# Low parts of the next stage's weights by accumulating transfers, and transposes moved later, in a float32 network of attention, delta-rule and feed-forward layers

## The chip, the cores and the metric

The kernel runs on one core of a Trainium2 chip. The metric is the device time of one execution in microseconds (us). The engines are PE (TensorE, matrix products), DVE (VectorE), ACT (ScalarE), POOL (GpSimd) and SP (SyncE, which only issues transfers here). Transfers are issued from SP's queue and from POOL's queue and run on the core's 16 DMA engines.

## What is computed

A small decoder over 512 tokens of width 1024, in float32. Two layers come first: a mixer (two kinds of attention in the first layer, differential attention in the second) and a feed-forward block with a gated convolution, each between two root-mean-square norms. Then come a gated delta-rule mixer, a squared-ReLU feed-forward block and a last norm.

```python
for layer in range(DEPTH):
    h = _rms_norm(x, norm_mix_pre[layer])
    m = _even_mixer(h, ...) if layer % 2 == 0 else _odd_mixer(h, ...)
    x = x + _rms_norm(m, norm_mix_post[layer])
    h = _rms_norm(x, norm_ffn_pre[layer])
    f = _conv_ffn(h, ffn_w_up[layer], ffn_conv_w[layer], ffn_conv_b[layer], ffn_w_down[layer])
    x = x + _rms_norm(f, norm_ffn_post[layer])
...
y = gated_deltanet(rms_norm(x, norm_mix), ...)
x = x + y
x = x + squared_relu_mlp(rms_norm(x, norm_mlp), mlp_w_up, mlp_w_down)
return rms_norm(x, norm_final)
```

## The kernel before

**Three products for one.** A float32 product is made of three products of parts: each operand is split into a high part (`hi`, the value cast to `fp32r`) and a low part (`lo`, the value less `hi`). `mm3` issues high by high, high by low, low by high, at lines 250 to 252; when the weight is the first operand, line 252 reads its low part and comes third.

**Weights.** `wtile` loads 128x1024 numbers (512 KB) into one of two buffers `raw` (`wload`, line 230, on SP's queue). `wsteps` then casts `raw` to `whi` on ACT (line 245) and makes `wlo = raw - whi` on DVE, or on POOL where `eng` says so (line 246). `whi` and `wlo` have four buffers each, used in turn. A buffer of `raw` can be loaded again when both the cast and the subtraction have read it.

**The five stage ends.** The tokens are four blocks t = 0 to 3 of 128. At the end of a stage each block is finished (norm and addition to x), scaled by the next norm (`scale`, a sum of squares on ACT; `rstd`, a power on POOL, line 265; `mul`, on DVE, line 293), transposed on PE (`turn`, line 301) and split into `hT`, high on ACT and low on DVE (`parts`). The next stage begins with a head: its first four weights W0 to W3, in `steps` that need only blocks 0 and 1. So PE works on the head while blocks 2 and 3 are made ready, and their `turn`s are put between the steps.

- `proj_out` ends the three mixers (even, odd, delta rule). Its head has 32 steps of three products, eight for each weight in turn, and `turn(2)` follows step 24, `turn(3)` step 29 (counted from 0). W0 and W3 get their low parts on POOL, W1 and W2 on DVE. W0 takes the buffers of the output projection's weight k=4, which is read last by the first two of the products of `block(3)`.
- `ffn_tail` ends the two gated feed-forward blocks. The down projection there is seven products of combined quarters (class `Seven`); products 3 to 6, each with two halves b of four `mm` (2.7 us of PE), are interleaved by hand with the norms. Its four weights come after product 6's first half, with low parts on DVE. Its head has 16 steps (first block) or 32 (second); `turn(2)` follows step 13 or 27, `turn(3)` the last. The residual is read back block by block (`reload`, SP's queue) into three buffers `scr`, which the scaled blocks use as well.

Around both the order of PE, ACT and DVE is the program's own (`manual_schedule`). SP's and POOL's orders are the planner's. Each engine works in order: an instruction that waits holds all behind it on its engine. Within class `Seven`, transfers on POOL's queue already add a quarter of the weights to another as they land (`accum_op=ALU.add`, line 96).

Of the kernel before, what the change touches and what calls it, by code (L numbers as in the profile page):

```python
# [10 lines left out]
F32 = mybir.dt.float32  # L11
F32R = mybir.dt.float32r
# [3 lines left out]
ALU = mybir.AluOpType  # L16
# [5 lines left out]
P = 128  # L22
# [115 lines left out]
def parts(hi, lo):  # L138

    return lambda k, t: (hi[:, k, t * P:(t + 1) * P], lo[:, k, t * P:(t + 1) * P])  # L140


class Kern:
# [92 lines left out]
    def wsplit(self, raw, n=1024, eng=None):  # L236
        parts, lo = self.wsteps(raw, n, eng)
        lo()
        return parts

    def wsteps(self, raw, n=1024, eng=None):

        hi = self.wp.tile([P, 1024], F32R, tag="whi", name="whi", bufs=4)
        lo = self.wp.tile([P, 1024], F32R, tag="wlo", name="wlo", bufs=4)
        self.nc.scalar.copy(hi[:, :n], raw[:, :n])  # L245
        return (hi, lo), lambda: (eng or self.nc.vector).tensor_tensor(lo[:, :n], raw[:, :n], hi.bitcast(F32)[:, :n], ALU.subtract)  # L246
# [27 lines left out]
    def scale(self, t):  # L274

        ss = self.sm([P, 1], "pn_ss")
        self.nc.scalar.activation(self.junk(), self.x[:, t, :], AF.Square, accum_out=ss)
        return self.rstd(ss, D, "pn_r")
# [90 lines left out]
    def proj_out(self, out, finish, nxt=None, tail=4):  # L369

        nc = self.nc
        nk = out.nk
        body = nk - tail
        lead = min(2, body)
        for h in (1, 0):
            for k in range(lead):
                for t in range(NT):
                    out.mm(k, t, h)  # L380
        for k in range(lead, body):
            for h in range(2):
                for t in range(NT):
                    out.mm(k, t, h)
        for k in range(body, nk):
            out.weight(k)
        order = [(k, h) for k in range(body, nk) for h in range(2)]

        def block(t, i0=0, i1=2 * tail):
            for k, h in order[i0:i1]:  # L390
                out.mm(k, t, h)

        banks = lambda t: (out.bank(0, t), out.bank(1, t))
        if not isinstance(nxt, tuple):
            for t in range(NT):
                if t:
                    order.sort(key=lambda kh: kh[1])
                block(t)
                if nxt:
                    nxt(t, banks(t))  # L400
                    continue
                for step in finish:
                    step(t, banks(t))
            return

        i, (srcs, run) = nxt
        f_scale, f_mul, f_add = (lambda t, f=f: f(t, banks(t)) for f in finish)
        E = mybir.EngineType
        scale, mul, turn, parts = self.prenorm(i)
        ws2 = []  # L410

        def weight(eng=None):
            if len(ws2) < len(srcs):
                ws2.append(self.wtile(*srcs[len(ws2)], eng=eng))

        with self.tc.manual_schedule(engines={E.PE, E.Activation, E.DVE}):
            block(0)
            f_scale(0)
            f_mul(0)
            block(1)  # L420
            f_add(0)
            scale(0)
            mul(0)
            f_scale(1)
            f_mul(1)
            f_add(1)
            block(2, 0, 3)
            turn(0)
            block(2, 3)
            parts(0)  # L430
            scale(1)
            mul(1)
            f_scale(2)
            f_mul(2)
            block(3, 0, 3)
            weight(nc.gpsimd)
            turn(1)
            block(3, 3)
            parts(1)
            weight()  # L440
            f_add(2)
            f_scale(3)
            scale(2)
            f_mul(3)
            weight()
            weight(nc.gpsimd)
            mul(2)
            f_add(3)
            scale(3)
            mul(3)  # L450
            steps = run(ws2)
            n = len(steps)
            for j, step in enumerate(steps):
                step()
                if j == n * 3 // 4:
                    turn(2)
                    parts(2)
                if j == n * 29 // 32:
                    turn(3)
                    parts(3)  # L460

# [860 lines left out]
    def ffn_tail(self, down, spare, put, xd, gain_row, nxt):  # L1322


        nc = self.nc
        i, (srcs, run) = nxt
        gain = self.gain(gain_row)
        E = mybir.EngineType
        scale, mul, turn, parts = self.prenorm(i, "bb")
        col = lambda h: slice(h * 512, h * 512 + 512)  # L1330
        ws2, xr, st = [], {}, {}

        def weight(eng=None):
            if len(ws2) < len(srcs):
                ws2.append(self.wtile(*srcs[len(ws2)], eng=eng))

        def reload(t):
            xr[t] = self.scr("xr")
            nc.sync.dma_start(xr[t], xd[:, t, :])

        def square(t, h):
            if t not in st:
                st[t] = self.sm([P, 2], "po_ss")
            nc.scalar.activation(self.junk()[:, col(h)], self.x[:, t, col(h)], AF.Square, accum_out=st[t][:, h:h + 1])

        def gained(t, h):
            nc.vector.tensor_tensor(self.x[:, t, col(h)], self.x[:, t, col(h)], gain[:, col(h)], ALU.mult)

        def half(t, h):
            square(t, h)  # L1350
            gained(t, h)

        def root(t):
            sum_ = self.sm([P, 1], "po_st")
            nc.vector.tensor_tensor(sum_, st[t][:, 0:1], st[t][:, 1:2], ALU.add)
            st[t] = self.rstd(sum_, D, "po_r")

        def add(t):
            nc.vector.scalar_tensor_tensor(self.x[:, t, :], self.x[:, t, :], st[t], xr[t], ALU.mult, ALU.add)

        def rest(b):

            put(*down.sums(5, b)[:2], 0, 1)

        def pairs(i, b, j0, j1):
            for j in range(j0, j1):
                down.mm(i, j, b)

        with self.tc.manual_schedule(engines={E.PE, E.Activation, E.DVE}):
            down.apart = True  # L1370
            down.weights(4)
            reload(0)
            reload(1)
            five, six = down.weights(5, spare[0]), down.weights(6, spare[1])
            for step in five:
                step()
            half(0, 0)
            down.block(3, 0)
            put(*down.sums(3, 0))
            down.block(4, 0)  # L1380
            put(*down.sums(4, 0))
            half(0, 1)
            six[0]()
            root(0)
            down.block(3, 1)
            put(*down.sums(3, 1))
            add(0)
            down.block(4, 1)
            put(*down.sums(4, 1))
            six[1]()  # L1390
            scale(0)
            half(1, 0)
            half(1, 1)
            mul(0)
            root(1)
            down.block(5, 0)
            put(*down.sums(5, 0))
            rest(0)
            add(1)
            down.block(5, 1)  # L1400
            turn(0)
            put(*down.sums(5, 1))
            parts(0)
            scale(1)
            reload(2)
            mul(1)
            rest(1)
            down.block(6, 0)
            weight()
            pairs(6, 1, 0, 2)  # L1410
            turn(1)
            pairs(6, 1, 2, 4)
            put(*down.sums(6, 0))
            parts(1)
            half(2, 1)
            weight()
            half(2, 0)
            root(2)
            reload(3)
            weight()  # L1420
            add(2)
            put(*down.sums(6, 1))
            half(3, 1)
            half(3, 0)
            root(3)
            scale(2)
            add(3)
            weight()
            mul(2)
            scale(3)  # L1430
            mul(3)
            steps = run(ws2)
            n = len(steps)
            for j, step in enumerate(steps):
                step()
                if j == n * 27 // 32:
                    turn(2)
                    parts(2)
                if j == n - 1:
                    turn(3)  # L1440
                    parts(3)
# [736 lines left out]
```

## Time and profile before

| | us |
|---|---|
| median of 3 runs (lowest, highest) | 1913.55 (1913.24, 1917.69) |
| the profiled execution, its own time | 1912.77 |
| its span in the trace | 1911.0 |
| PE busy (share of the span) | 1869.3 (98%) |
| DVE busy | 1229.3 (64%) |
| ACT busy | 906.1 (47%) |
| POOL busy | 314.1 (16%) |

The span is the time from the first to the last instruction in the trace. Busy time is a sum over instructions, and PE's ends are modelled. Times in the rows below count from the span's start. In a timeline a row has the start, the duration, the engine, the line, the operation with its output and inputs, its shape, how many were merged, and in brackets how long the engine sat idle before it and what ended that. The even mixer ends near 300 us, the first feed-forward block near 645 us, the odd mixer near 885 us, the second feed-forward block near 1240 us and the delta-rule mixer near 1586 us.

### The profile page before, as it was taken

What the parts mean: (1) busy time and instruction counts of PE and PEld (TensorE: products, weight loads), DVE (VectorE), ACT (ScalarE), POOL (GpSimd) and SP (SyncE); (2) the same over time, 40 slices, a digit from 0 to 9 for tenths busy, and PEclk for the clock granted to TensorE, in tenths of its full rate; (3) what the DMA queues carried; (4) which work ended last, traced back from release to release, by engine and by line L of the source; (5) the groups of instructions that cost most, each with busy time, mean ns of one, the idle gap of its engine ahead of it and who ended that gap; (6) DMA issues with size and microseconds to landing.
All of it is one profiled execution on the core that took longest, in us unless ns stands there. A gap on an engine that the chain in (4) does not pass through costs nothing.

```text
span 1911.0 us, 25424 instructions
## 1 busy us (share of the span) xinstructions
PE 1869.3 (98%) x9732; PEld 1542.6 (81%) x9732; DVE 1229.3 (64%) x1959; ACT 906.1 (47%) x1453; POOL 314.1 (16%) x412
## 2 busy tenths in 40 slices
PE   7999999999999999999999999999999999999998
PEld 6778688888888788878888888788778879888886
DVE  5666656565657647847555666877763747766767
ACT  4665644343434546645343344476622424444444
POOL 0212420100101223412010100100264311100101
PEclk9999999999999999999999999999999999999999
DMA  5212146453734321127363543523330146746553
GB/s 175 63 52 82 45 147 211 105 190 94 183 109 78 129 68 57 65 89 249 103 190 110 128 160 80 151 84 101 97 98 4 45 132 203 194 111 198 125 140 88
DMA packets 66046, 226.01 MB, mean 118 GB/s; under 512 B 8788, under 2 KB 9684, under 8 KB 65796
## 3 DMA queue, kind: packets, MB, share of 16 engines
q1 hardware_dynamic: 52948, 181.77, 27.8%
q0 software_dynamic: 12976, 42.61, 12.7%
q8 instruction: 77, 1.26, 0.3%
q14 instruction: 45, 0.37, 0.1%
HBM read 214.32 MB, written 9.96 MB: 117 GB/s over the span
## 4 chain that ended last, share of the span: by engine, by line
PE 51%; DVE 3%; ACT 1%; issue 1%; DMA 1%; POOL 1%; POOLq 0%; ACTq 0%; DVEq 0%
PE up L250 3%; PE up L251 3%; PE up L252 3%; PE X L250 2%; PE X L251 2%; PE X L252 2%; PE dproj L250 2%; PE gate L252 2%; PE val L252 2%; PE gate L251 2%; PE val L251 2%; PE gate L250 2%; PE val L250 2%; PE dproj L251 2%; PE dproj L252 2%; PE Z L251 1%
## 5 line engine op out<-in xcount | busy, mean ns | idle before, releaser
L246 DVE TENSOR_TENSOR wlo<-raw,whi 128x1024 fp32r<-128x1024 f32 (+2 forms) x205 | 250.9, 1228 | 170.0 <-ACT whi L245 163.6
L245 ACT CAST whi<-raw 128x1024 fp32r<-128x1024 f32 (+3 forms) x225 | 234.0, 1042 | 239.6 <-PE gate L251 54.1
L245 ACT CAST whi<-quarter 128x1024 fp32r<-128x1024 f32 (+1 forms) x132 | 132.6, 1008 | 182.9 <-PE X L252 48.6
L246 DVE TENSOR_TENSOR wlo<-quarter,whi 128x1024 fp32r<-128x1024 f32 (+1 forms) x132 | 153.4, 1166 | 89.7 <-ACT whi L245 89.3
L96 POOL DMA_DIRECT2D quarter<-in_ff_wq x48 | 41.7, 880 | 590.0 <-DVE wlo L246 480.4
L250 PE MATMUL gate<-hhi,whi 128*128 128x512 f32 x320 | 124.5, 389 | 0.0
L251 PE MATMUL gate<-hlo,whi 128*128 128x512 f32 x320 | 124.5, 389 | 0.0
L252 PE MATMUL gate<-hhi,wlo 128*128 128x512 f32 x320 | 124.5, 389 | 0.0
L250 PE MATMUL val<-hhi,whi 128*128 128x512 f32 x320 | 124.5, 389 | 0.0
L251 PE MATMUL val<-hlo,whi 128*128 128x512 f32 x320 | 124.5, 389 | 0.0
L252 PE MATMUL val<-hhi,wlo 128*128 128x512 f32 x320 | 124.5, 389 | 0.0
L226 DVE TENSOR_TENSOR mlo<-q,mhi 128x1792 fp32r<-128x1792 f32 x38 | 77.0, 2026 | 58.3 <-ACT mhi L225 58.3
L250 PE MATMUL X<-whi,mhi 128*128 128x512 f32 x272 | 106.1, 390 | 0.0
L251 PE MATMUL X<-wlo,mhi 128*128 128x512 f32 x272 | 105.8, 389 | 0.0
L252 PE MATMUL X<-whi,mlo 128*128 128x512 f32 x272 | 105.4, 389 | 0.0
L225 ACT CAST mhi<-q 128x1792 fp32r<-128x1792 f32 x38 | 64.4, 1696 | 77.7 <-DVE q L1928 67.1
L250 PE MATMUL up<-hhi,whi 128*128 128x512 f32 x224 | 87.1, 389 | 0.0
L251 PE MATMUL up<-hlo,whi 128*128 128x512 f32 x224 | 87.1, 389 | 0.0
L252 PE MATMUL up<-hhi,wlo 128*128 128x512 f32 x224 | 87.1, 389 | 0.0
L252 PE MATMUL head<-hhi,wlo 128*128 128x256 f32 (+1 forms) x256 | 73.0, 287 | 1.9 <-DVE wlo L246 1.5
L250 PE MATMUL head<-hhi,whi 128*128 128x256 f32 (+1 forms) x256 | 71.9, 287 | 1.3 <-ACT whi L245 1.0
L251 PE MATMUL head<-hlo,whi 128*128 128x256 f32 (+1 forms) x256 | 72.7, 285 | 0.1
(461 smaller groups left out, 4856.1 us busy)
## 6 DMA issues: line engine op xcount, KB each, us to landing
raw<-in_ff_wup SPq DMA_DIRECT2D x88, 512.0 KB, 3.5
quarter<-in_ff_wq SPq DMA_DIRECT2D x40, 512.0 KB, 5.2
quarter<-in_ff_wq POOLq DMA_DIRECT2D x40, 512.0 KB, 5.5
raw<-in_ml_wup SPq DMA_DIRECT2D x32, 512.0 KB, 3.5
quarter<-in_ml_wdown SPq DMA_DIRECT2D x32, 512.0 KB, 6.4
quarter<-in_ml_wdown POOLq DMA_DIRECT2D x32, 512.0 KB, 5.5
raw<-in_dn_wqkv SPq DMA_DIRECT2D x24, 512.0 KB, 3.7
raw<-in_od_wqk SPq DMA_DIRECT2D x16, 512.0 KB, 3.4
```

Of the source, the lines that this page charges most:

```text
L96: self.K.nc.gpsimd.dma_start(r[quarter][:, :src[other].shape[-1]], src[other], accum_op=ALU.add)
L225: i = self.nc.scalar.copy(hi, src)
L226: return i.ins, (eng or self.nc.vector).tensor_tensor(lo, src, hi.bitcast(F32), ALU.subtract).ins
L245: self.nc.scalar.copy(hi[:, :n], raw[:, :n])
L246: return (hi, lo), lambda: (eng or self.nc.vector).tensor_tensor(lo[:, :n], raw[:, :n], hi.bitcast(F32)[:, :n], ALU.subtract)
L250: mm(out, lhs[0], rhs[0], start=start, stop=False, **kw)
L251: mm(out, lhs[0], rhs[1], start=False, stop=False, **kw)
L252: return mm(out, lhs[1], rhs[0], start=False, stop=stop, **kw)
```

## The change

A new function `wtile_dma` makes a weight's low part without a subtraction on an engine: ACT casts `raw` to `hi`, ACT writes `-hi` into `lo`, and a transfer on POOL's queue adds the weight, read from memory a second time, onto `lo` as it lands. `raw` is then free as soon as the cast has read it. `proj_out` uses it for W0 and W3, in place of POOL's subtraction; `ffn_tail` uses it for all four weights, in place of DVE's, and calls for them earlier (W0 after `root(0)`, W1 after block 1's squares, W2 after `add(1)`, W3 after `rest(1)`). In `proj_out`, `turn(2)` moves from step 24 to step 27 and `turn(3)` from step 29 to step 31, the last. In `ffn_tail`, one `mm` of product 6 more stands ahead of `turn(0)`, and one more ahead of `turn(1)`, so that one `mm` in place of two follows it.

```diff
+    def wtile_dma(self, src, n=1024):
+
+        raw = self.wload(src, n)
+        hi = self.wp.tile([P, 1024], F32R, tag="whi", name="whi", bufs=4)
+        lo = self.wp.tile([P, 1024], F32R, tag="wlo", name="wlo", bufs=4)
+        self.nc.scalar.copy(hi[:, :n], raw[:, :n])
+        self.nc.scalar.mul(lo[:, :n], hi.bitcast(F32)[:, :n], -1.0)
+        self.nc.gpsimd.dma_start(lo[:, :n], src, accum_op=ALU.add)
+        return hi, lo
+
@@ proj_out
-        def weight(eng=None):
+        def weight(make=self.wtile):
             if len(ws2) < len(srcs):
-                ws2.append(self.wtile(*srcs[len(ws2)], eng=eng))
+                ws2.append(make(*srcs[len(ws2)]))
...
             block(3, 0, 3)
-            weight(nc.gpsimd)
+            weight(self.wtile_dma)
             turn(1)
             block(3, 3)
             parts(1)
...
             weight()
-            weight(nc.gpsimd)
+            weight(self.wtile_dma)
             mul(2)
             f_add(3)
...
-                if j == n * 3 // 4:
+                if j == n * 27 // 32:
                     turn(2)
                     parts(2)
-                if j == n * 29 // 32:
+                if j == n - 1:
                     turn(3)
                     parts(3)
@@ ffn_tail
-        def weight(eng=None):
+        def weight():
             if len(ws2) < len(srcs):
-                ws2.append(self.wtile(*srcs[len(ws2)], eng=eng))
+                ws2.append(self.wtile_dma(*srcs[len(ws2)]))
...
             half(0, 1)
             six[0]()
             root(0)
+            weight()
             down.block(3, 1)
...
             half(1, 0)
             half(1, 1)
+            weight()
             mul(0)
             root(1)
             down.block(5, 0)
             put(*down.sums(5, 0))
             rest(0)
             add(1)
+            weight()
             down.block(5, 1)
+            pairs(6, 0, 0, 1)
             turn(0)
             put(*down.sums(5, 1))
             parts(0)
...
             reload(2)
             mul(1)
             rest(1)
-            down.block(6, 0)
             weight()
-            pairs(6, 1, 0, 2)
+            pairs(6, 0, 1, 4)
+            pairs(6, 1, 0, 3)
             turn(1)
-            pairs(6, 1, 2, 4)
+            pairs(6, 1, 3, 4)
             put(*down.sums(6, 0))
             parts(1)
             half(2, 1)
-            weight()
             half(2, 0)
             root(2)
             reload(3)
-            weight()
             add(2)
...
             add(3)
-            weight()
             mul(2)
```

## Rows read from the trace of the kernel before

**Rows 1.** Windows of the span: busy times of each engine, clock, DMA share, GB/s.

```profile
300.00:600.00 300.00, 300.00 (x1331) 248.52 (x1330) 182.08 (x216) 124.38 (x135) 18.13 (x21) 1.00 0.49 134
```

**Rows 2.** Waits of PE over the span: total us, times, longest us.

```profile
PE pn_t L301 <- DVE nrm L293: 15.0, 9, 7.9
...
PE head L252 <- DVE wlo L246: 1.5, 1, 1.5
...
PE head L250 <- ACT whi L245: 1.0, 1, 1.0
```

**Rows 3.** Timeline of PE at the end of the first feed-forward block.

```profile
619.10 1.09 PE L301 MATMUL pn_t<-ident,nrm 128*128 128x128 f32 x8 [0.34 <-DVE nrm L293]
...
625.70 1.07 PE L301 MATMUL pn_t<-ident,nrm 128*128 128x128 f32 x8 [1.39 <-DVE nrm L293]
...
637.89 0.50 PE L250 MATMUL headb<-whi,hhi 128*128 128x512 f32 x1 [1.49 <-ACT whi L245]
639.90 0.67 PE L251 MATMUL headb<-wlo,hhi 128*128 128x512 f32 x1 [1.51 <-DVE wlo L246]
```

**Rows 4.** Windows around the low clock at the two feed-forward ends (columns of rows 1).

```profile
637.00:643.00 6.00, 3.61 (x11) 2.70 (x12) 4.94 (x6) 1.99 (x3) 1.44 (x3) 0.76 0.55 186
1232.00:1238.00 6.00, 4.04 (x21) 3.84 (x22) 4.95 (x5) 1.89 (x4) 1.00 (x2) 0.72 0.75 303
```

**Rows 5.** Timelines of ACT and DVE at the even mixer's end.

```profile
270.54 1.06 ACT L245 CAST whi<-raw 128x1024 fp32r<-128x1024 f32 x1 [0.67 <-PE o L252]
...
280.66 1.05 ACT L245 CAST whi<-raw 128x1024 fp32r<-128x1024 f32 x1 [2.10 <-DMA raw<-in_ff_wup]
...
273.88 1.28 DVE L246 TENSOR_TENSOR wlo<-raw,whi 128x1024 fp32r<-128x1024 f32 x1 [0.31 <-ACT whi L245]
```

**Rows 6.** Timeline of PE at the even mixer's end.

```profile
275.55 0.28 PE L252 MATMUL head<-hhi,wlo 128*128 128x256 f32 x1
...
284.82 0.38 PE L252 MATMUL head<-hhi,wlo 128*128 128x256 f32 x1 [0.47 <-POOL wlo L246]
...
288.27 1.09 PE L301 MATMUL pn_t<-ident,nrm 128*128 128x128 f32 x8 [0.40 <-DVE nrm L293]
```

**Rows 7.** POOL's 30 accumulating transfers of 512 KB between 1610 and 1900 us.

```profile
DMA to landing us min/median/max: 5.3/5.5/8.5
```

**Rows 8.** POOL's accumulating transfers issued in 283:287 and 1581:1583 (last column: us to landing).

```profile
quarter<-in_ff_wq POOLq DMA_DIRECT2D x1, 512.0 KB, 9.5
...
quarter<-in_ml_wdown POOLq DMA_DIRECT2D x1, 512.0 KB, 9.7
```

**Rows 9.** Timelines of ACT, DVE, POOL and PE at the odd mixer's end.

```profile
874.69 1.05 ACT L245 CAST whi<-raw 128x1024 fp32r<-128x1024 f32 x1 [0.96 <-DMA raw<-in_ff_wup]
...
876.11 3.42 DVE L334 SCALAR_TENSOR_TENSOR x<-post,po_rr,x 128x1024 f32<-128x1024 f32 x1
...
875.82 2.63 POOL L246 TENSOR_TENSOR wlo<-raw,whi 128x1024 fp32r<-128x1024 f32 x1 [3.09 <-ACT whi L245]
...
869.88 0.28 PE L252 MATMUL head<-hhi,wlo 128*128 128x256 f32 x1
...
883.05 1.09 PE L301 MATMUL pn_t<-ident,nrm 128*128 128x128 f32 x8 [1.50 <-DVE nrm L293]
```

**Rows 10.** Timelines of ACT and PE at the delta-rule mixer's end.

```profile
1578.57 1.05 ACT L245 CAST whi<-raw 128x1024 fp32r<-128x1024 f32 x1 [1.95 <-DMA raw<-in_ml_wup]
...
1573.49 0.28 PE L252 MATMUL head<-hhi,wlo 128*128 128x256 f32 x1
```

**Rows 11.** Timelines of ACT and DVE at the end of the first feed-forward block.

```profile
616.39 0.63 ACT L1344 ACTIVATE junk<-x 128x512 bf16<-128x512 f32 x1
...
624.26 1.28 DVE L293 SCALAR_TENSOR_TENSOR nrm<-x,pn_rr,gain 128x1024 f32<-128x1024 f32 x1 [0.72 <-POOL pn_rr L265]
...
639.76 1.28 DVE L293 SCALAR_TENSOR_TENSOR nrm<-x,pn_rr,gain 128x1024 f32<-128x1024 f32 x1
```

**Rows 12.** The page's DMA issues: SP's plain loads of `raw` (last column: us to landing).

```profile
raw<-in_ff_wup SPq DMA_DIRECT2D x88, 512.0 KB, 3.5
```

## The prediction

> **What bounds the kernel now.** I read the windows by stage first. Inside a feed-forward block PE is busy for all of 300 us while ACT and DVE have room [rows 1]: PE sets the end, and a change pays only where PE stands still or runs at its low clock. The list of PE's waits then says how much there is to win: the waits of `turn` for scaled blocks are the largest, and the head's weights come next [rows 2]. PE's timeline places them. In the first feed-forward end there are four: 0.34 and 1.39 before `turn(0)` and `turn(1)`, 1.49 and 1.51 before the high and the low part of W3 [rows 3]. The second has 0.34, 1.39, 1.03 and 1.46 (the last two in [rows 2]). The mixers' ends have 0.47 and 0.40 (even [rows 6]), 1.50 (odd [rows 9]) and none (delta rule). After the two late waits of a feed-forward end the granted clock is 0.76 and 0.72 over 6 us [rows 4], so part of that stretch runs at the lower of the two levels (1.2 of 2.4 GHz): 6 x 0.24 = 1.4 and 6 x 0.28 = 1.7 us more. All that the change can win is so 4.7 + 1.4, 4.2 + 1.7, 0.9 and 1.5: some 14 us.
>
> **The change at the feed-forward ends.** Removed: four DVE subtractions, of which three stand in the chain to blocks 2 and 3. Added: four ACT multiplications (priced as the cast of the same tile, 1.05 us [rows 5]), four POOL transfers. The casts move forward. W0's waits for nothing, since the buffers of product 3 are free by then. W1 and W2 (4 x 1.05 = 4.2 us of ACT) start after block 1's squares at 617.1 [rows 11] and end near 621.3, ahead of `parts(0)`. So the sum of squares of block 1 starts about 0.5 us later, but DVE is busy with `hlo` until nearly then; I put `nrm(1)` 0.1 later than its 625.55 [rows 11]. PE, with one `mm` (0.68) moved ahead of `turn(0)`, has no wait there, and gets to `turn(1)` at 624.5 (619.4, transposes 0.8, six `mm` and a start of 0.1 to 0.2): 1.2 us of waiting are left. The last transfer is issued near 625.6 and lands 5.5 later [rows 7], at 631.1; its step is reached near 635.8, so low parts are in time. What is late next is block 2: without three subtractions (3 x 1.2) its `mul` ends near 637.9 in place of 641.0 [rows 11], against 637.2 for PE (`turn(1)` at 625.8, transposes and one `mm` 1.6, 14 steps of 0.7), a wait of 0.7; block 3 leaves 0.1. So the first end goes from 4.7 + 1.4 = 6.1 to 2.0, the second, by the same steps, from 5.9 to 1.5 (PE gets to `turn(2)` later there, after 28 narrower steps). Together 8.5 us won. Bounds: 9.5, if `turn(1)` waits 0.7 in each; 6.5, if W1's transfer goes ahead of block 1's power on POOL (0.9 us of issue) and lengthens both waits. Queued behind the waiting transfers on POOL are only powers of squares that ACT computes later anyway.
>
> **The change at the mixers' ends.** Here W0 is cast at 270.54, when `block(3)` lets its buffers go [rows 5], and PE wants its low part at 275.55 as the third product of the head [rows 6]. POOL's subtraction fitted into these 5.0 us. The new chain is cast 1.06, multiplication 1.05, transfer 5.5 [rows 7]: 278.15, so PE waits 2.6 us. The odd and the delta-rule end have the same distance from cast to product, and their products at 869.88 and 1573.49 [rows 9, 10] wait as long: 3 x 2.6 = 7.8. The least of the 30 transfers behind the 5.5 took 5.3 [rows 7]. The Trainium skill (DMA: Bandwidth & Descriptors, Anatomy of one DMA) fits a transfer from GpSimd's queue as 2.0 us plus its bytes at 436 GB/s, an estimate of 3.2 us for 512 KB. By that PE would wait 0.3 here, and the whole sum would come to about -2; the rows here are accumulating transfers like the new ones, and I go by them.
>
> W3 comes later still. Its `raw` is W1's, free when DVE has W1's low part (273.88 plus 1.28 [rows 5]); ACT's new multiplication before `parts(1)` puts that off by 0.9. W3's casts stood at 280.66, 874.69 and 1578.57 [rows 5, 9, 10]; with 0.9, cast and multiplication the transfers are issued at 283.6, 877.7 and 1581.6. Load is what makes this price unknown: POOL's transfers took 5.5 in a quiet stage [rows 7], but 9.5 and 9.7 when issued in these ends, among the next stage's loads [rows 8]. I take 7.5, the middle, because W3's are issued somewhat before those. They land at 291.1, 885.2 and 1589.1. PE would want them 8.64 us after W0's (24 steps of 0.36): at 284.2, 878.5, 1582.1. So PE is late by 6.9, 6.7 and 7.0 us in all, whatever part of it was already lost at W0 or to a low clock after it. At 5.5 it is 4.9, 4.7 and 5.0; at 9.5, 8.9, 8.7 and 9.0.
>
> The clock comes on top only after the second wait. Its price is 1.4 to 1.7 for 3.0 us of waiting [rows 3, 4]; here a wait of about 2.7 is left after 2.6 + 1.5, so I put 0.75, half, between nothing and 1.5. `turn(3)` after the last step has no step to cover `parts(3)`: 0.3 each, between nothing and the 0.5 of a cast half as wide as that of 1.05 [rows 5], whose end the next product needs. What goes: 0.47 and 0.40, which the new wait contains, and odd's 1.50. That one came from DVE's addition of 3.42 us, which overlapped POOL's subtraction of 2.63 [rows 9]; a DVE instruction on as many elements takes 1.28 [rows 5]. With POOL's subtraction gone, so is that delay.
>
> Sum: 20.6 + 2.25 + 0.9 - 2.4 = 21.4 lost, 8.5 won: 12.9 us more. The profiled execution took 1912.77, 0.8 under the median of runs, so about 1926.
>
> The DMA engines get 14 transfers more, at places where a wait is priced already. Later loads have more time, since PE comes later; in the feed-forward blocks PE has no wait to lengthen [rows 1].
>
> **The rivals.**
> *W3 is in time.* W1's and W2's loads no longer go out together, and a plain load lands in 3.5 us where it is alone [rows 12], some 2 us sooner than I let W3's `raw` land. Its transfer at 5.5 then makes PE late by 2.9, 2.7 and 3.0, and what W0 costs with the clock after it, 2.6 + 1.5 = 4.1, contains that: 12.3 + 0.9 - 2.4 - 8.5 = 2.3: 1915, no change that can be measured. The quiet stage speaks for it, the loaded transfers [rows 8] against. The rule cited above ends on the same side, near 1911. 0.2.
> *The ends cost nearly nothing.* As above, and the low parts land in 3.5 as plain loads do [rows 12]: W0 costs 0.6, W3 0.9, 0.7 and 1.0, which contain it; no fall of the clock. 2.6 + 0.9 - 2.4 - 8.5 = -7.4: 1906, faster. It decides from the point where PE loses less than 1.4 us in each end. Against it speaks that no transfer of the 30 was as quick [rows 7]. 0.1.
> *The feed-forward ends win nothing.* If SP's queue has `reload(3)`, which waits for `scr` until block 1 is added (near 621.7), ahead of W2's load, W2's cast stands before `parts(0)` and holds it for some 4 us; the win is gone: 21.4, 1934. In the queue's order before, loads followed the program's order, which speaks against it. 0.1.
> *The change as I read it*: 1926, with 1918 to 1935 as its own range. 0.6.
>
> **How the numbers follow.** Slower by over 0.3% (5.7 us, about what a measurement of this kernel tells from no change): main case and third rival, 0.7; within it 0.2; faster 0.1. The range leaves out the fast rival and the top of the slow cases: 1911 to 1935.
>
> **What would show it.** At the mixers' ends: the first product of line 252 of the head waits about 2.6 us for a transfer, the one 24 steps later again 1 to 4 us, with a granted clock under 1 in between, and no wait before `turn(2)` or `turn(3)`. At the feed-forward ends: no wait for a weight, a clock of 1, about 1.2 us before `turn(1)` and under 1 before `turn(2)`. The forecast is wrong if the transfers of W0 land within 4 us of their issue, if W3's land before PE has done its 24 steps, or if a cast on ACT at the feed-forward ends waits for its load.

## The result and the profile after

The changed kernel took 1946.12 us (median of 4 runs; the kernel before 1913.79 beside it): 1.0157 times as long, interval 1.0141 to 1.0174, so 30 us slower by this ratio (32 by the medians) where 12.9 were forecast, and outside the range. One of the four executions took 3617 us (without it the median is 1945.77); it is left out of the ratio and of all comparisons below. The profile shown is that of `e1_changed`, the same kernel once more: 1943.45 us, span 1941.6, 30.7 more than the 1912.77 of the profiled execution before. Its lines are 10 higher than those of before (250 to 252 are 260 to 262, 301 is 311, 293 is 303).

To see where the 30.7 us came from, I read when PE reaches `turn(0)` at each of the five ends. First the timeline of PE before, without the row of the first feed-forward end, which stands in [rows 3]:

```profile
264.70 1.03 PE L301 MATMUL pn_t<-ident,nrm 128*128 128x128 f32 x8
...
859.02 1.04 PE L301 MATMUL pn_t<-ident,nrm 128*128 128x128 f32 x8
1213.88 1.09 PE L301 MATMUL pn_t<-ident,nrm 128*128 128x128 f32 x8 [0.34 <-DVE nrm L293]
1562.63 1.03 PE L301 MATMUL pn_t<-ident,nrm 128*128 128x128 f32 x8
```

and the same in the changed kernel:

```profile
266.60 1.04 PE L311 MATMUL pn_t<-ident,nrm 128*128 128x128 f32 x8
625.62 1.03 PE L311 MATMUL pn_t<-ident,nrm 128*128 128x128 f32 x8
868.86 1.03 PE L311 MATMUL pn_t<-ident,nrm 128*128 128x128 f32 x8
1233.11 1.09 PE L311 MATMUL pn_t<-ident,nrm 128*128 128x128 f32 x8
1578.72 1.03 PE L311 MATMUL pn_t<-ident,nrm 128*128 128x128 f32 x8
```

The differences of the starts, with the `mm` of 0.68 us that now stands ahead of `turn(0)` at the feed-forward ends put back, give each stretch its loss:

| from | forecast | measured |
|---|---|---|
| start to the even end | 0 | +1.90 |
| even end on | +7.1 | +3.94 |
| first feed-forward end on | -4.1 | +4.00 |
| odd end on | +6.3 | +8.71 |
| second feed-forward end on | -4.4 | -2.46 |
| delta rule's end on | +8.1 | +14.59 |
| sum | +12.9 | +30.68 |

So the mixers' ends lose 27.2 instead of 21.4, and the feed-forward ends, which should have won 8.5, lose 1.5. The 1.9 us ahead of the first edit are no part of the change (last section). Nor are 2.6 us of the row "second feed-forward end on": it runs through the whole delta-rule mixer, and near that mixer's end the delay falls from 18.66 us, at an output product (first row of each pair), to the 16.09 at `turn(0)`. Of the kernel before:

```profile
1536.92 0.50 PE L250 MATMUL o<-whi,gp 128*128 128x512 f32 x1 [0.34 <-ACT gp L1911]
...
1545.00:1562.00 17.00, 15.00 (x59) 11.68 (x58) 6.64 (x8) 3.24 (x4) 0.55 (x1) 0.90 0.42 143
```

and of the changed kernel:

```profile
1555.58 0.50 PE L260 MATMUL o<-whi,gp 128*128 128x512 f32 x1 [0.34 <-ACT gp L1922]
...
1561.00:1578.00 17.00, 16.05 (x70) 12.64 (x69) 8.18 (x10) 3.67 (x5) 0.55 (x1) 1.00 0.51 171
```

PE waits there for weights of the mixer itself, 1.25 and 0.76 us before and 0.53 and 0.42 after, and the granted clock is 0.90 and 1.00. The change has no line there, and in the ten other kernels of this document the first of these waits is anything from 0.37 to 2.33 us. Without the 2.6 us the feed-forward ends lose some 4.

**The mixers' ends.** The timeline of PE, answering to [rows 6, 9, 10]; the first row of each pair is the first product with W0's low part, the second that with W3's:

```profile
280.47 0.58 PE L262 MATMUL head<-hhi,wlo 128*128 128x256 f32 x1 [2.85 <-DMA wlo<-in_ff_wup]
...
291.13 0.39 PE L262 MATMUL head<-hhi,wlo 128*128 128x256 f32 x1 [0.49 <-DMA wlo<-in_ff_wup]
...
1593.59 0.39 PE L262 MATMUL head<-hhi,wlo 128*128 128x256 f32 x1 [3.84 <-DMA wlo<-in_ml_wup]
...
1611.32 0.58 PE L262 MATMUL head<-hhi,wlo 128*128 128x256 f32 x1 [7.34 <-DMA wlo<-in_ml_wup]
```

(At the odd end they start at 883.06 and 896.96, after waits of 3.15 and 3.52.) The timeline of POOL has the issues that these products wait for:

```profile
274.91 0.95 POOL L248 DMA_DIRECT2D wlo<-in_ff_wup  x1 [1.40 <-ACT wlo L247]
...
284.31 0.91 POOL L248 DMA_DIRECT2D wlo<-in_ff_wup  x1 [3.29 <-ACT wlo L247]
...
887.58 0.91 POOL L248 DMA_DIRECT2D wlo<-in_ff_wup  x1 [4.29 <-ACT wlo L247]
...
1597.24 0.90 POOL L96 DMA_DIRECT2D quarter<-in_ml_wdown  x1 [4.09 <-DMA quarter<-in_ml_wdown]
1597.86 1.18 POOL L248 DMA_DIRECT2D wlo<-in_ml_wup  x1
```

From issue to product W0 took 5.6 us at the even end. W3 took 6.8, 9.4 and 13.5 at the three ends: the same instruction with the same bytes, and at the last end it stood behind one of `Seven`'s accumulating transfers on POOL's queue. Of the clock, windows around the arrival of W3 at the odd and the delta rule's end (columns as in [rows 1]):

```profile
896.00:903.00 7.00, 6.04 (x38) 5.98 (x38) 1.38 (x2) 1.40 (x3) 0.00 (x0) 0.76 1.04 341
...
1610.00:1617.00 7.00, 5.68 (x36) 5.69 (x37) 1.29 (x2) 1.08 (x2) 0.47 (x1) 0.67 0.56 118
```

That is at most 7 x 0.24 = 1.7 and 7 x 0.33 = 2.3 us more; each window begins with about 1 us of the wait itself, in which a low clock costs nothing. At the even end, after a wait of 0.49, the window 290 to 297 has 1.00. Behind W0's waits the clock falls at all three ends: 0.76 over 279 to 286, 0.72 over 883 to 889 and 0.76 over 1593 to 1600.

**The feed-forward ends.** No product waits for a weight any more, as forecast. What is late is `turn`. The first end, on PE, DVE and SP:

```profile
632.58 1.06 PE L311 MATMUL pn_t<-ident,nrm 128*128 128x128 f32 x8 [1.83 <-DVE nrm L303]
...
649.75 1.94 PE L311 MATMUL pn_t<-ident,nrm 128*128 128x128 f32 x8 [5.87 <-DVE nrm L303]
...
642.64 0.15 DVE L982 TENSOR_SCALAR sub<-sub 128x1 f32<-128x1 f32 x1 [5.96 <-DMA sub<-in_od_subln]
642.72 1.29 DVE L1369 SCALAR_TENSOR_TENSOR x<-x,po_rr,xr 128x1024 f32<-128x1024 f32 x1
...
626.40 4.62 SPq L230 DMA_DIRECT2D raw<-in_od_wqk  x2
631.07 0.85 SPq L1349 DMA_DIRECT2D xr<-xf  x1
631.97 0.56 SPq L981 DMA_DIRECT2D sub<-in_od_subln  x1
```

(The eight transposes of `turn(2)` took 1.94 us in place of 1.06: after 5.87 us of standing still the granted clock is 0.54 over 649 to 656.) The wait before `turn(2)` is not made by the norm's chain. DVE stood still for 5.96 us in front of `sub`, 128 numbers of the next stage that are scaled once, with `add(2)` right behind it. The planner has put this instruction in among the end's own, a place that costs nothing if the load has landed by then. Before, it had: SP issued `sub` at 627.68, it landed 3.3 us later, and DVE came to it at 631.40. Now SP's queue stands for 4.6 us at two loads of the next weights, the second of which waits for a buffer `raw`, and `sub` goes out at 631.97 and takes 10.7 us beside transfers of 512 KB. At the second end two casts of `seln` (2 KB) on ACT do the same to `scale(2)`: 2.26 us, behind three such loads at which SP stands for 7.5.

### The profile page after: what moved, and what is told of

Read it like the earlier page. It is cut to its first block, busy times and chain, and to the rows that moved or that the text cites. A ratio compares the mean times of both kernels' runs of the same rounds, so it can differ in the third digit from the quotient of the medians.

```text
span 3615.6 us, 25452 instructions
## 1 busy us (share of the span) xinstructions
PE 3595.0 (99%) x9732; PEld 2359.5 (65%) x9732; DVE 1213.0 (34%) x1951; ACT 932.2 (26%) x1467; POOL 305.7 (8%) x420
## 3 DMA queue, kind: packets, MB, share of 16 engines
q8 instruction: 77, 1.26, 0.1%
## 4 chain that ended last, share of the span: by engine, by line
PE 99%; DMA 1%; issue 0%; DVE 0%; ACT 0%; POOL 0%; SPq 0%; POOLq 0%; DVEq 0%
PE val L260 4%; PE gate L260 4%; PE gate L261 4%; PE gate L262 4%; PE val L261 4%; PE val L262 4%; PE X L262 3%; PE X L261 3%; PE X L260 3%; PE up L262 2%; PE up L261 2%; PE up L260 2%; PE o L260 2%; PE o L261 2%; PE o L262 2%; PE dproj L260 2%
## 5 line engine op out<-in xcount | busy, mean ns | idle before, releaser
L255 ACT CAST whi<-raw 128x1024 fp32r<-128x1024 f32 (+2 forms) x211 | 218.6, 1039 | 699.2 <-PE gate L261 200.9
L260 PE MATMUL val<-hhi,whi 128*128 128x512 f32 x320 | 215.9, 675 | 0.0
L262 PE MATMUL val<-hhi,wlo 128*128 128x512 f32 x320 | 215.9, 675 | 0.0
L262 PE MATMUL gate<-hhi,wlo 128*128 128x512 f32 x320 | 215.9, 675 | 0.0
L1292 DVE TENSOR_TENSOR q<-q,val 128x512 f32<-128x512 f32 x40 | 27.5, 688 | 318.9 <-PE val L262 318.9
L260 PEld LDWEIGHTS gate<-hhi,whi 128*128 128x128 f32 x320 | 95.7, 299 | 54.1 <-issue 50.6
L262 PEld LDWEIGHTS val<-hhi,wlo 128*128 128x128 f32 x320 | 95.1, 297 | 54.7 <-issue 51.2
L260 PEld LDWEIGHTS val<-hhi,whi 128*128 128x128 f32 x320 | 95.6, 299 | 53.8 <-issue 49.9
L262 PEld LDWEIGHTS gate<-hhi,wlo 128*128 128x128 f32 x320 | 95.5, 298 | 53.9 <-issue 50.2
L261 PEld LDWEIGHTS gate<-hlo,whi 128*128 128x128 f32 x320 | 95.5, 299 | 53.5 <-issue 49.8
L261 PEld LDWEIGHTS val<-hlo,whi 128*128 128x128 f32 x320 | 94.8, 296 | 54.3 <-issue 50.6
```

Of the source, the lines that this page charges most:

```text
L260: mm(out, lhs[0], rhs[0], start=start, stop=False, **kw)
L261: mm(out, lhs[0], rhs[1], start=False, stop=False, **kw)
L262: return mm(out, lhs[1], rhs[0], start=False, stop=stop, **kw)
L1292: nc.vector.tensor_tensor(c, c, pv, ALU.mult)
```

## The experiments

All were timed beside the kernel before; "x" is the ratio to it.

**The change in parts.** `e1_changed` is the change. `e2_mixer_ends_only` has `proj_out` alone, `e3_ff_ends_only` `ffn_tail` alone, and `e4_turns_only` the moved transposes and `mm` alone, with the low parts on the engines as before.

> The changed kernel itself, to have a profile of it at full clock. Theory A (as forecast, only larger): the loss of 32 us lies at the three mixers' ends, where PE waits for the low parts of W0 and W3; PE's waits on transfers of wlo there sum to 20 us or more, and the feed-forward ends show none. Theory B: the feed-forward ends lose too, with new waits there for a weight or a cast that waits for its load.

> The change in the three mixers' ends alone, the feed-forward ends as before. Theory A: about 40 us more than before (32 and the 8 that the feed-forward ends win). Theory B: 15 to 25 us more.

> The change in the two feed-forward ends alone, the mixers' ends as before. Theory A: 8 us less than before. Theory B: 5 to 15 us more.

> Only the moves in PE's order (turns later at all five ends), with low parts made on DVE and POOL as before. Both theories: within 3 us of before; the waits before a turn get 1 to 2 us shorter in sum, those for a weight stay.

| | us (median) | x, interval |
|---|---|---|
| before, in this job | 1914.78 | |
| e1_changed | 1947.04 | 1.0175, 1.0157 to 1.0194 |
| e2_mixer_ends_only | 1945.52 | 1.0161, 1.0143 to 1.0180 |
| e3_ff_ends_only | 1918.14 | 1.0017, 1.0008 to 1.0027 |
| e4_turns_only | 1917.08 | 1.0010, 1.0000 to 1.0020 |

Neither theory has it: the mixers' ends cost 31 us, between the two, and the feed-forward ends win nothing and lose 3. The moved transposes alone are worth nothing within the measurement.

**Why the feed-forward ends don't win.** `e5_smalls_kept` is `e3_ff_ends_only` with three small instructions held in the program's order, and SP's and POOL's orders unchanged:

```diff
-        nc.vector.tensor_scalar(sub, sub, 1.0 - LAMBDA_INIT, None, ALU.mult)
+        self.tc.keep_in_program_order(nc.vector.tensor_scalar(sub, sub, 1.0 - LAMBDA_INIT, None, ALU.mult))
...
-        nc.scalar.copy(st["sel"], seln[0:40, :])
+        self.tc.keep_in_program_order(nc.scalar.copy(st["sel"], seln[0:40, :]))
...
-        nc.scalar.copy(st["selb"], seln)
+        self.tc.keep_in_program_order(nc.scalar.copy(st["selb"], seln))
```

> The changed feed-forward ends with the mixers' ends as before, and three small instructions of the next stage (the scaling of sub on DVE, the two casts of seln on ACT) kept in program order, behind the norms of blocks 2 and 3. Theory Q (in e3_ff_ends_only the 6.0 us of waiting before turn(2) in the first end, and 2.2 in the second, come from these instructions, which wait on their engine for loads of 0.5 and 2 KB that SP issues behind loads of 512 KB): both waits fall under 1 us, and the time is 6 to 9 us below that of e3_ff_ends_only, about 1910, some 4 us below the kernel before. Rival C (the weights' casts, multiplications and transfers make blocks 1 and 2 late by themselves, the small load only ends last): another wait takes the place, turn(2) still waits 4 us or more, and the time stays within 2 us of 1918.

`e6_root_first` adds:

```diff
-        with self.tc.manual_schedule(engines={E.PE, E.Activation, E.DVE}):
+        with self.tc.manual_schedule(engines={E.PE, E.Activation, E.DVE, E.Pool}):
...
             half(1, 1)
-            weight()
             mul(0)
             root(1)
+            weight()
```

> e5_smalls_kept with POOL in program order in the feed-forward ends and W1 made behind root(1), so that the power of block 1 is ahead of the issue of W1's transfer on POOL. Theory P (that issue, 0.9 us, puts the power, add(1), scale(1) and so turn(1) off by 0.8): the wait before turn(1) falls from 2.1 and 2.2 us to 1.3 and 1.4, and the time by 1.5 to 2 against e5_smalls_kept. Rival H (the casts of W1 and W2 on ACT ahead of parts(0) hold turn(1)): the wait before turn(1) stays at 2.1 and 2.2, and the time within 0.5 us of e5_smalls_kept.

Measured: `e5_smalls_kept` 1906.77 (before 1913.89), x 0.9963, 0.9951 to 0.9976; `e6_root_first` 1904.85, x 0.9953, 0.9940 to 0.9966. Theory Q holds, and these waits cost more than it said: `e5_smalls_kept` is 11.4 us below `e3_ff_ends_only` in the medians (10.5, each against the kernel before beside it), where 6 to 9 were expected. In PE's timeline of `e5_smalls_kept` `turn(2)` comes without a wait at the first and the second end:

```profile
639.66 1.04 PE L311 MATMUL pn_t<-ident,nrm 128*128 128x128 f32 x8
...
1230.27 1.06 PE L311 MATMUL pn_t<-ident,nrm 128*128 128x128 f32 x8
```

Nothing about the weights was changed for it. Theory P holds in PE's timeline of `e6_root_first`, which has the wait before `turn(1)` at both ends:

```profile
625.71 1.06 PE L311 MATMUL pn_t<-ident,nrm 128*128 128x128 f32 x8 [1.26 <-DVE nrm L303]
...
1215.88 1.06 PE L311 MATMUL pn_t<-ident,nrm 128*128 128x128 f32 x8 [1.25 <-DVE nrm L303]
```

It was 2.04 and 2.22 in `e5_smalls_kept`. POOL's timeline of `e1_changed` shows what stood in front of the power (second end, where `turn(1)` waited 2.86):

```profile
1234.30 0.92 POOL L248 DMA_DIRECT2D wlo<-in_dn_wqkv  x1 [3.38 <-ACT whi L246]
1234.91 0.90 POOL L275 TENSOR_TENSOR po_rr<-po_ru,mhalf 128x1 f32<-128x1 f32 x1
```

DVE had `po_ru` ready at 1233.3. In the times the two kernels' intervals overlap, so that the 1.9 us between them are shown by the waits alone.

**W0 or W3.** In `e7_w3_transfer` only W3's low part comes by transfer at the mixers' ends, in `e8_w0_transfer` only W0's; the other is POOL's subtraction as before, `turn`s late, `ffn_tail` as before:

```diff
@@ e7_w3_transfer: first weight of proj_out (e8_w0_transfer: the fourth)
-            weight(self.wtile_dma)
+            weight(lambda src, n=1024: self.wtile(src, n, nc.gpsimd))
```

> Mixers' ends: W0's low part by POOL's subtraction as before, W3's by transfer; turns late as in the change; feed-forward ends as before. Theory L (W3's late landing sets the end, and what PE loses at W0 is contained in it): 27 to 31 us above the kernel before, as e2_mixer_ends_only, with waits for W3 of about 5, 8 and 13 us. Theory S (the losses at W0 and W3 add up): the three waits at W0 and the low clock behind them go, 12 to 15 us, and 15 to 19 us are left.

> Mixers' ends: W0's low part by transfer, W3's by POOL's subtraction as before; turns late as in the change; feed-forward ends as before. Theory L: three waits of 2.9, 3.2 and 3.8 us for W0 and 1.4 us of low clock behind each, no wait for W3: 12 to 15 us above the kernel before, so that this run's loss and that of e7_w3_transfer add up to far more (about 42) than that of e2_mixer_ends_only (31). Theory S: they add up to the 31. If W0 alone costs under 5 us, the later product gives most of it back, and neither theory has its size.

Measured beside 1913.89: 1945.50 (x 1.0166, 1.0152 to 1.0180) and 1926.41 (x 1.0067, 1.0054 to 1.0080). W3 alone costs all of the mixers' loss, 31.6 us; W0 alone 12.5, and adding it to W3 costs nothing more. The waits of PE over the whole of `e7_w3_transfer`, total, times, longest:

```profile
PE head L262 <- DMA wlo<-in_ff_wup: 17.1, 2, 8.6
...
PE head L262 <- DMA wlo<-in_ml_wup: 8.2, 1, 8.2
```

and of `e8_w0_transfer`:

```profile
PE head L262 <- DMA wlo<-in_ff_wup: 6.0, 2, 3.1
...
PE head L262 <- DMA wlo<-in_ml_wup: 4.5, 1, 4.5
```

Theory L holds, but not with the sizes that I had given its three waits (5, 8 and 13): without W0's wait ahead of it W3 took 9.4 to 9.8 us at all three ends, and at the last one its transfer now stood ahead of `Seven`'s on POOL's queue. That its loss and that of `e2_mixer_ends_only` agree within 1 us owes something to chance: PE's waits on these transfers sum to 8.2 us here against 10.4 there at the last end, and to 17.1 against 13.8 at the other two.

**Is it the load?** `e9_w3_loads_held` is `e7_w3_transfer` with the first quarters' loads later in SP's queue and the `reload` of blocks 0 and 1 in program order there, `e10_root_first_held` the same on `e6_root_first`:

```diff
+            if keep:
+                self.K.tc.keep_in_program_order(i)
...
@@ reload
-            nc.sync.dma_start(xr[t], xd[:, t, :])
+            i = nc.sync.dma_start(xr[t], xd[:, t, :])
+            if t < 2:
+                self.tc.keep_in_program_order(i)
...
@@ first Seven of conv_ffn (of mlp: j in (2, 3), load(j - 2))
-                    if j % 2 == 0:
-                        down.load(j // 2)
+                        if j in (1, 2):
+                            down.load(j - 1, True)
```

> e7_w3_transfer (W3's low part by transfer at the mixers' ends, W0's by POOL) with the loads of the first product's quarters held back in SP's queue, behind the next weights of up; at the delta rule's end only two loads of 512 KB are then left beside W3's transfer, at the even and odd ends gains, xr and weights fill part of the gap. Theory D (the landing of 9.4 to 9.8 us that e7_w3_transfer showed comes from the loads that share the DMA engines): at the delta rule's end the transfer lands 5.5 to 7 us after its issue and PE waits about 5 us in place of 8.3; at the other two ends 0 to 2 us less; the time falls by 3 to 8 us, to about 1940. Rival F (these transfers are slow by themselves, through their destination or POOL's queue): the landing at the delta rule's end stays at 9 us or more and the time within 2 us of e7_w3_transfer.

> e6_root_first (the feed-forward ends of the change with both repairs, mixers' ends as before) with the same loads held back. Theory D: W3's raw comes sooner at the mixers' ends and the waits left there (0.5 and 0.4, 1.5, 0.4) shrink: 0 to 2 us below e6_root_first. Rival: the held quarters come late for their first product, or the gains and xr that fill the gap cost as much; 0 to 5 us above it.

`e9_w3_loads_held` took 1945.92 (before 1914.57), x 1.0162, 1.0142 to 1.0183, with a landing of 9.5 us at the delta rule's end. By its expectation that is the rival's case, but the experiment had missed its aim: SP stood until 1604.56 at a load of weights, and then issued the four quarters around W3's transfer (1605.03). At the even and odd ends gains, `xf` and `xr` took the quarters' place; there W3's transfer landed after 11.7 and 10.4 us, where `e7_w3_transfer` has 9.4 and 9.8 and theory D had 0 to 2 less, although the DMA share while it was under way had fallen, from 1.03 at both to 0.82 and 0.90. So the share alone does not give the landing; what else does, no run shows. `e10_root_first_held` took 1902.80, x 0.9938, 0.9924 to 0.9952: the lowest median here, 12 us below the kernel before. Its interval overlaps that of `e6_root_first`, so the held loads are not shown to be worth anything by themselves. `e11_w3_quiet` moves all eight quarters of the last block behind the fourth step of `up`:

```diff
@@ first Seven of mlp
-                    if j % 2 == 0:
-                        down.load(j // 2)
+                        if j == 3:
+                            down.load(0, True)
+                            down.load(1, True)
```

> e7_w3_transfer with the eight loads of the last block's first quarters moved in SP's queue behind the weights of the fourth step of up, so that beside W3's transfer at the delta rule's end only two plain loads of 512 KB move (in e9_w3_loads_held four quarters still went out within 0.5 us of that transfer, and it landed after 9.5). The even and odd ends are as in e7_w3_transfer. Theory D (load on the DMA engines makes the landing): 5.5 to 7.5 us from issue to landing at the delta rule's end in place of 9.8, and PE waits 4 to 6 us in place of 8.3. Rival F (the transfer is that slow by itself): landing 9 us or more, PE waits 8. The time as a whole says less, since the held quarters may come late for their product.

Now the transfer lands 7.0 us after its issue at 1600.50, and PE waits 5.08 (1938.90 us, x 1.0123, 1.0094 to 1.0152). The windows from 1597 to 1612 us of `e7_w3_transfer`

```profile
1597.00:1612.00 15.00, 6.75 (x43) 6.55 (x42) 2.57 (x4) 2.57 (x5) 2.46 (x3) 0.73 1.03 325
```

and of `e11_w3_quiet`

```profile
1597.00:1612.00 15.00, 9.92 (x67) 9.71 (x66) 5.24 (x7) 4.07 (x6) 1.55 (x2) 0.77 0.41 108
```

differ in the DMA share, 1.03 against 0.41. Theory D holds at this end for what lies above 7 us in these kernels: 2.8 of the 9.8 of `e7_w3_transfer`, and 2.5 of the 9.5 of `e9_w3_loads_held`, where four quarters but no transfer of `Seven`'s stood beside W3's. The 13.4 us of `e1_changed` lie 3.6 higher still; there W3's transfer stood behind `Seven`'s on POOL's queue, in `e7_w3_transfer` ahead of it, and no run changes that order alone. Nor does one explain the 1.5 us from the quiet 5.5 [rows 7] to 7.0. At the even and odd ends no run took the load away.

## Why the prediction was wrong

The direction was right, and so was most of the arithmetic at the mixers' ends. Three steps failed, two at the feed-forward ends and one at the mixers'.

**"Feed-forward ends win 8.5."** The chain to blocks 2 and 3 did get shorter by what I had counted: with the small instructions out of the way (`e5_smalls_kept`) the ends win 7.1 us in the medians, and with the power ahead of the issue (`e6_root_first`) 9.0, with `turn(1)` waiting 1.26 and 1.25 where I had forecast 1.2, and `turn(2)` nothing where I had 0.7. What I did not look at was what else stands in DVE's and ACT's queues between the instructions I moved, and which loads feed it. `sub` is in the timeline of before, at 631.40 on DVE; I counted it at nothing since it took 0.15 us and waited for nothing. It waited for nothing because its load, issued at 627.68, had landed 0.4 us earlier. The weights made earlier free `raw` earlier, the next weights' loads move up, and SP's queue stands at them. The third rival had the right queue (SP's) and the right price (the win is gone), but another victim: I let the queue hold W2's load and with it `parts(0)`; it held a load of 0.5 KB. I gave it 0.1.

**"Queued behind the waiting transfers on POOL are only powers of squares that ACT computes later anyway."** Wrong for block 1's own power, by 0.8 us at the first end and 1.0 at the second (the waits before `turn(1)` in `e5_smalls_kept` less those in `e6_root_first`). I had this as the lower bound (6.5) and put the value without it.

**The landing of W3, "I take 7.5".** The term that was mis-sized. The issues came where I had them: 13.1, 12.8 and 13.1 us after W0's cast by the forecast, 11.9, 12.8 and 13.3 measured (casts at 272.45, 874.74 and 1584.57). From issue to product the transfers took 6.8, 9.4 and 13.5. With PE wanting W3 13.65 us after that cast (5.01 to W0's product, 8.64 more), it is late by 5.0, 8.6 and 13.1, together 26.7 in place of 20.6; with the other terms as forecast (2.25 + 0.9 - 2.4) that makes 27.5, and 27.2 were measured. So the even end came out better than its 6.9 and the delta rule's nearly twice as bad as its 7.0. My reason for the middle, that W3's transfer is issued somewhat before `Seven`'s, held at the even end (2.9 us before) and the odd (2.7), and failed at the delta rule's, where `Seven`'s went out 0.6 us ahead of it. My range for the landing ended at 9.5, the two loaded transfers of [rows 8]. Those show one of these in flight; the change puts a second one beside it. The transfers of `e1_changed` from 1590 to 1615 us, by queue (SP's in the first row, POOL's in the second; packets, MB, share of the 16 engines):

```profile
q1 hardware_dynamic: 1452, 5.27, 53.1%
q0 software_dynamic: 570, 2.07, 44.8%
```

53.1 / 5.27 = 10.1% of the engines' time for each plain MB, 44.8 / 2.07 = 21.6% for each accumulating one: a low part that comes this way takes twice the engines' time of the load that it repeats, and together they fill the stretch. (Over 1650 to 1850 us of the kernel before, POOL's 9.26 MB took 26.6% and SP's 22.02 MB 31.6%: twice as much for each MB there too.) The Trainium skill (DMA: Bandwidth & Descriptors, Issuing engines are not separate DMA queues) says that transfers of all issuing engines run on the same 16 DMA engines and interleave. The 9.5 and 9.8 against 7.0 us at the delta rule's end agree with it, and I had weighed POOL's transfers as if the stage's own loads were a fixed background.

**What held.** That W0's wait is contained in what W3 costs (`e7_w3_transfer` against `e2_mixer_ends_only`); its size, 2.6 forecast, 2.9 to 4.5 measured (`e1_changed` and `e8_w0_transfer`); the second fall of the clock after W3's wait, at the odd and the delta rule's end though not at the even; no weight late at the feed-forward ends of the changed kernel (in `e6_root_first` one is, by 0.51 us, after a transfer of 10.8 us where I had 5.5); `turn(2)` and `turn(3)` without a wait at the mixers' ends. *W3 is in time* and *the ends cost nearly nothing* both needed W3's transfer to land within 5.5 us; the quickest took 6.8.

The two sides add up: against the forecast the mixers' ends lost 5.8 us more, the feed-forward ends 10.0 (12.6, less the 2.6 in the delta-rule mixer), and 1.9 lie ahead of the first edit: 17.8 before rounding, from 12.9 to 30.7.

## What to carry to other kernels

When an edit lets loads start earlier, follow the issuing queue past the edit to the next small load behind them, and find the instruction of the next stage that consumes it: if it stands among the ones you are speeding up, it sets their time. Price a transfer on the path by what else is in flight where it lands, the edit's own transfers included, and not by its quiet duration. An accumulating transfer in place of an engine's subtraction pays where the product is wanted late, as at the feed-forward ends here (0.9953 with both repairs; the earlier calls for the weights came with it and were not tried without it), and loses where it is wanted soon and the stage's loads go out at that moment: at the mixers' ends PE wanted W3's low part 13.65 us after W0's cast, and the transfer was issued 11.9 to 13.3 us after it.

## What was not expected of the hardware

**A clock that falls or not after the same wait.** Between 200 and 240 us, ahead of the first edit, PE waits once for 1.9 us in all kernels. The windows of the kernel before and of `e1_changed` there:

```profile
200.00:240.00 40.00, 38.11 (x208) 25.97 (x207) 25.64 (x57) 26.01 (x69) 12.16 (x9) 1.00 0.13 43
```

```profile
200.00:240.00 40.00, 38.11 (x203) 25.89 (x201) 25.33 (x55) 24.49 (x65) 12.54 (x9) 0.96 0.15 46
```

Same wait, same busy time of PE, and a granted clock of 1.00 or 0.96 over 40 us, 1.6 us of work at the higher of its two levels. Five of the twelve profiles have 0.96: `e1_changed`, `e2_mixer_ends_only`, `e3_ff_ends_only`, `e10_root_first_held` and `e11_w3_quiet`. The changed kernel's `turn(0)` then starts 1.9 us later; in `e10_root_first_held`, whose order there is that of `e6_root_first`, it starts at 266.79, in `e6_root_first` at 264.61. So one execution's span can differ by 2 us in a stretch that no edit touches. What decides it stays open.

**Small loads beside large ones.** 0.5 KB for `sub` took 3.3 us from issue to landing before, and 10.7 behind and beside transfers of 512 KB.
